# An encoder layer on one core: one ring of eight PSUM banks from the merge on, instead of rings of six and two

## The chip, the cores and the metric

The kernel runs on one core of one Trainium2 chip. The metric is the device time of one execution in microseconds (us); smaller is better. TensorE (PE in the profile) multiplies matrices and can write only to PSUM, which on this core is divided into eight banks of 128 partitions by 512 fp32 values. VectorE (DVE) and ScalarE (ACT) read the banks out; GpSimd (POOL) works on what they have put into SBUF; SyncE (SP) issues the DMA transfers. Each engine works through its own queue in order, and waits at the head of that queue for what its next instruction needs.

## The reference

One encoder layer is applied to two sequences of 512 tokens with 1024 features, with one set of weights, and a last normalization follows. Cut to the parts that matter here:

```python
def _rmsnorm(x, g):
    xf = x.astype(jnp.float32)
    y = xf * lax.rsqrt(jnp.mean(xf * xf, axis=-1, keepdims=True) + EPS)
    return (y * g.astype(jnp.float32)).astype(x.dtype)

def _layer(x, mem, l, p):
    xn = _rmsnorm(x, p['norm_mix'][l])
    ...                                   # S5 scan, differential attention, cross attention
    for n in range(N_BRANCH):
        term = jax.nn.sigmoid(g[..., n * D_MODEL:(n + 1) * D_MODEL]) * (branches[n] @ p['w_up'][l, n])
        merged = term if merged is None else merged + term
    x = x + merged @ p['w_out'][l]
    xn2 = _rmsnorm(x, p['norm_ffn'][l])
    gate, up = jnp.split(xn2 @ p['w_ffn_in'][l], 2, axis=-1)
    return x + (jax.nn.silu(gate) * up) @ p['w_ffn_out'][l]

def _trunk(x, mem, p):
    ...
    return _rmsnorm(x, p['norm_final'])
```

All is fp32, the feed-forward width is 2816, and the result is the normalized x of both sequences.

## The kernel before

**Products.** Features lie on the partitions and tokens on the free axis. Every fp32 operand is split into a high and a low part (`split`: a rounded copy on ScalarE and a subtraction on VectorE, L134 and L135), and a product is the sum of three matmuls per block of 128 features: high by high, high by low, low by high. The sum is collected in one PSUM bank. All matmuls are issued at L66, all transposes (a small matrix by the identity) at L69.

**The stages after the attention.** From L929 on stand, in this order: the merge of the second sequence (`merge_units`), the out projection (`out_tile`, which also sums up the squares of the new x for the second norm), the feed-forward input product in 22 tiles of 128 columns of gate and of up (i from 0 to 21), the feed-forward output product in visits (the loop over `VISITS`), and an end part with the last rows of that product.

**A tile and a visit.** Both form two by two quadrants from seven products in place of eight. A tile from 1 to 20 forms its seven products one after the other, 12 matmuls each, each in a bank of its own. Tile 0 gets its operands piece by piece, so it opens six banks at once and forms a seventh product, `last`, behind them. Tile 21 and every visit open seven banks at once. In `quadrants` the banks are read in the order of the products: a copy on ScalarE (L1108), then additions on VectorE (`summed`, L1102) into u2, c11, u3, p1, c22, c21 and c12; the fifth product's bank is read twice. For a tile, c11 and c12 are called gf, c21 and c22 up.

**The norm of the feed-forward input** is applied behind the product. In tile 0, `rstd` (L186) sums the squares of each sequence over the partitions with matmuls against a column of ones into a bank `ss`; `factor` (L195) takes the square root on ScalarE (L198) and the reciprocal on VectorE (L199), and four transposes spread the result over a bank `bc`. `S.copy` (L1155) copies it into `accs[s]`, by which the tile's quadrants are multiplied (L1164 on VectorE, L1166 on GpSimd).

**The end part** (L1334 to L1370) goes over three groups of columns: the 512 tokens of the first sequence, then the first and the second half of the second. For each, eight products m = 0 to 7 are added to y (L1346), the squares are collected in `acc` (ScalarE L181; the addition at L182 on GpSimd, for the last m on VectorE), `column_sums` gives `ss` with matmuls against ones, and `final` (L1314) calls `factor` and multiplies y by the result. The last group sums m = 5, 6 and 7 straight from the squares (L1360).

**The banks.** `open_banks` closes the rings that are open and opens new ones; `bank(tag)` takes the next bank of a ring, and a first write into it waits for the readers of what was in it before. From L929 to the end there are two rings: "mm" of six banks for products, and "tr" of two, from which `aux()` takes a bank for `ss`, for `bc`, and for the seventh product of tile 21 and of each visit.

**Order.** A scheduler orders the instructions of each engine within the program by the data they need, by what its own estimates say is ready, and by the order in which a ring hands out its banks. While `PE.on` is true the matmuls keep the order in which they are written: that is so from tile 21 through the visits; in the tiles before, and in the end part, the scheduler chooses.

Of the kernel before, what the change touches and what calls it, by code (L numbers as in the profile page):

```python
# [72 lines left out]
def encoder(ctx: ExitStack, tc: tile.TileContext, a, out):  # L73
# [14 lines left out]
    def open_tags(es, side=None, **tags):  # L88

        for tag, n in tags.items():  # L90
            pools[tag] = es.enter_context(tc.tile_pool(name=tag, bufs=n, side=side, reuse_waits="tile"))

    def open_banks(**tags):

        bank_es.close()
        for tag, n in tags.items():
            pools[tag] = bank_es.enter_context(tc.tile_pool(name=tag, bufs=n, space=PSUM, reuse_waits="tile"))

    bank_es = ExitStack()

    open_tags(ctx, ld=4)
    xp_es, phase = ExitStack(), ExitStack()
# [6 lines left out]
    def bank(tag="mm"):  # L109
        return pools[tag].tile([P, 512], F32, tag=tag, name="bk" + tag)  # L110

    def aux():
        return bank("tr")


    ident = cst.tile([P, P], F32, name="ident")
# [14 lines left out]
    def split(hi, lo, src, scale=None):  # L131

        if scale is None:
            h = S.copy(hi, src)  # L134
            l_ = V.tensor_tensor(out=lo, in0=src, in1=hi.bitcast(F32), op=ALU.subtract)  # L135
        else:
            h = S.activation(out=hi, in_=src, func=AF.Copy, scale=scale)
            l_ = V.scalar_tensor_tensor(out=lo, in0=src, scalar=scale, in1=hi.bitcast(F32), op0=ALU.mult, op1=ALU.subtract)
        return h, l_
# [65 lines left out]


    open_banks(mm=4, tr=4)
    bD = drp.tile([3, 4, P, NT], F32, name="bD")
    gD = drp.tile([24, P, NT], F32, name="gD")
# [83 lines left out]
    def queued():  # L293

        return tc.issue_after(last_w.ins)
# [146 lines left out]
    def raw_in(raw, m, p, whole=True):  # L442

        f = slice(2 * p * P, (2 * p + 2) * P)
        nc.sync.dma_start(raw[:, 1:3], a["w_fo"][m, :, f].rearrange("p (a n) -> p a n", n=P))
        if whole:
            return nc.sync.dma_start(raw[:, 0::3], a["w_fo"][m + 4, :, f].rearrange("p (a n) -> p a n", n=P))
        f = slice((2 * p + 1) * P, (2 * p + 2) * P)
        return nc.sync.dma_start(raw[:, 3], a["w_fo"][m + 4, :, f])

    def raw_sums(raw):

        a21, a11, a12, a22 = (raw[:, i] for i in range(4))
        PO.tensor_tensor(out=a22, in0=a21, in1=a22, op=ALU.add)  # L454
        PO.tensor_tensor(out=a21, in0=a11, in1=a21, op=ALU.subtract)
        PO.tensor_tensor(out=a11, in0=a22, in1=a11, op=ALU.subtract)
        PO.tensor_tensor(out=a12, in0=a12, in1=a11, op=ALU.subtract)

    def prepare(es_, todo_):
        pq = es_.enter_context(tc.tile_pool(name="pq", bufs=1, side="right", reuse_waits="tile"))  # L460
        raws = []

        def load():
            if len(raws) < len(todo_):
                raws.append(pq.tile([P, 4, P], F32, tag="raw", name="raw", bufs=4))
                with queued():
                    raw_in(raws[-1], *todo_[len(raws) - 1][:2])

        def part(n_, j, w_):
            m, p, _ = todo_[n_]  # L470
            k = w_.shape[1]
            hl = pq.tile([P, k, 2, P], F32R, tag=f"hl{k}", name="hl", bufs=k // 2)
            split(hl[:, :, 0], hl[:, :, 1], w_, scale=0.5)
            nc.sync.dma_start(wD[m, p][:, j : j + k], hl.bitcast(F32))

        for _ in range(3):
            load()
        yield
        for n_, (m, p, k) in enumerate(todo_):
            load()  # L480
            if k == 7:
                part(n_, 4, raws[n_][:, 1:4])
            if k == 7 or n_ == 0:
                raw_sums(raws[n_])
                yield
            part(n_, 0, raws[n_])
            if n_ + 1 < len(todo_) and todo_[n_ + 1][2] == 4:
                raw_sums(raws[n_ + 1])
            yield
# [201 lines left out]
    for i in range(-AHEAD, len(steps) + 1):  # L691
# [14 lines left out]
        if 0 <= i < len(steps):  # L706
# [4 lines left out]
            tr = aux()  # L711
# [214 lines left out]
    ves.close()  # L926


    open_banks(mm=6, tr=2)  # L929
    open_tags(phase, ms=16)  # L930
    ves = ExitStack()
    open_tags(ves, z=6)
# [21 lines left out]
    def out_tile(m, s, w):  # L954
        cs = slice(s * L, (s + 1) * L)
        xr = slot("xr", [P, L], name="xr")
        nc.sync.dma_start(xr, a["xT"][s, :, m, :])
        ps = bank()
        for k in range(KD):
            mm3([ps], w[0], w[1], [(mgh[k][:, cs], mgl[k][:, cs])], k, KD)  # L960
        V.tensor_tensor(out=x1[m][:, cs], in0=ps, in1=xr, op=ALU.add)
        nc.sync.dma_start(x1D[m, :, cs], x1[m][:, cs])
        sum_sq(accs[s], x1[m][:, cs], m == 0)
# [39 lines left out]
    def weights4(i):  # L1003

        nonlocal last_w
        a1, a2 = (wp.tile([P, DM], F32, tag="wf", name="wf") for _ in range(2))
        nc.sync.dma_start(a1, a["w_fg"][i])
        last_w = nc.sync.dma_start(a2, a["w_fu"][i])
        res = {}

        def sp(pool, src, sfx, *names):
            n = len(names) * H
            nonlocal last_s
            wh, wl = (pool.tile([P, DM], F32R, tag=t_ + sfx, name=t_, bufs=2) for t_ in ("wh", "wl"))
            last_s = split(wh[:, :n], wl[:, :n], src)
            for j, nm in enumerate(names):
                res[nm] = (wh[:, j * H : (j + 1) * H], wl[:, j * H : (j + 1) * H])

        sp(wp, a1, "", "A11", "A12")
        sp(wp, a2[:, H:], "", "A22")  # L1020
        yield res
        s12, s34 = (slot("ld", name="ws") for _ in range(2))
        PO.tensor_tensor(out=s12[:, :H], in0=a2[:, :H], in1=a2[:, H:], op=ALU.add)
        PO.tensor_tensor(out=s12[:, H:], in0=s12[:, :H], in1=a1[:, :H], op=ALU.subtract)
        PO.tensor_tensor(out=s34[:, H:], in0=a1[:, H:], in1=s12[:, H:], op=ALU.subtract)
        PO.tensor_tensor(out=s34[:, :H], in0=a1[:, :H], in1=a2[:, :H], op=ALU.subtract)
        yield
        sp(aps, s12, "s", "S1", "S2")
        sp(aps, s34, "s", "S3", "S4")
        yield  # L1030
# [12 lines left out]
    for s in range(NS):  # L1043
        for m, w in zip((3, 7), ws):
            out_tile(m, s, w)
    phase.close()
    open_tags(phase, th1=2, tl1=2)
    w0 = weights4(0)
    res0 = next(w0)
# [68 lines left out]
    def act_pair(p, tag="ts", third=PO):  # L1118

        xa_, xb_ = slot("ld", name="fa"), slot("ld", name="fb")  # L1120
        nc.sync.dma_start(xa_, aD[2 * p])
        nc.sync.dma_start(xb_, aD[2 * p + 1])
        return xa_, xb_, quad_sums(xa_, xb_, tag, third)

    def all7(i):
        wg = weights4(i)
        with yielding(last_q):
            w = next(wg)
        with tc.issue_after(last_p.ins):
            for _ in wg:  # L1130
                pass
        return w

    nxt_w = res0
    for i in range(KFF):
        w = nxt_w or all7(i)
        nxt_w = None
        if i == 1:
            prep = prepare(pes, pieces[NPREP[0] : NPREP[1]])
            next(prep)  # L1140
        elif i == KFF - 3:
            assert next(prep, None) is None
            pes.close()
            open_tags(fes, side="right", tsa=1, tsb=1)
        if i == KFF - 1:
            with tc.issue_after(last_s[1].ins):
                acts = [act_pair(0, "tsa"), act_pair(1, "tsb", V)]
            PE.on = True

        ps = products(i, w)  # L1150
        p0 = next(ps)
        if i == 0:
            for s in range(NS):
                _, bc = rstd(accs[s], DM)
                S.copy(accs[s], bc)  # L1155
        gf0, gf1, up0, up1 = quadrants(ps, p0)
        ac = ap2.tile([P, NT], F32, tag="ac", name="ac")
        with ExitStack() as es_:
            if i == KFF - 2:
                nxt_w = all7(i + 1)  # L1160
                es_.enter_context(tc.issue_after(last_s[1].ins))
            for s, gf, up in ((0, gf0, up0), (1, gf1, up1)):
                cs = slice(s * L, (s + 1) * L)
                V.tensor_tensor(out=gf, in0=gf, in1=accs[s], op=ALU.mult)  # L1164
                last_t = S.activation(out=ac[:, cs], in_=gf, func=AF.Tanh, scale=0.5)  # L1165
                PO.tensor_tensor(out=up, in0=up, in1=accs[s], op=ALU.mult)  # L1166
                V.scalar_tensor_tensor(out=ac[:, cs], in0=ac[:, cs], scalar=1.0, in1=gf, op0=ALU.add, op1=ALU.mult)
                V.tensor_tensor(out=ac[:, cs], in0=ac[:, cs], in1=up, op=ALU.mult)
        nc.sync.dma_start(aD[i], ac)
        if 1 <= i < KFF - 3:  # L1170
            half_piece((last_t, last_sum))
# [621 lines left out]
```

## Time and profile before

| | us |
|---|---|
| median of 3 runs | 1599.68 |
| lowest and highest | 1599.19, 1600.62 |
| the profiled execution, own time | 1599.28 |
| the profiled execution, span | 1597.5 |

The profile shows one execution. Its span runs from the first to the last instruction; 1.78 us of that execution's time lie around it. A time in a row of the profile counts from the start of the span. A row of the timeline gives the start, the duration, the engine, the line, the operation with its output and inputs, their sizes, how many instructions the row stands for, and in brackets how long the engine had been idle before it and what ended that. A matmul's duration includes its passage through the array, so that matmuls overlap: what one costs in a row of them is the distance between two starts.

### The profile page before, as it was taken

The numbers are of one execution on the slowest core, as the hardware profiler recorded it, in microseconds if no ns is written. First come the engines' busy times: TensorE is split into PE (matmuls) and PEld (weight loads), VectorE is DVE, ScalarE is ACT, GpSimd is POOL, SyncE is SP. The second block draws the span as 40 slices with busy tenths as digits, with TensorE's granted clock in tenths as the row PEclk, the third lists the DMA queues.
The fourth block names the chain that finished last, engine by engine and source line by source line (L and its number), as shares of the span: only waits on it lengthen the run. The fifth ranks groups of instructions, "written<-read, shape, count | busy, mean of one in ns | idle before, by whom it ended". The sixth has DMA issues, their size and how long they took to land.

```text
span 1597.5 us, 21606 instructions
## 1 busy us (share of the span) xinstructions
PE 1579.1 (99%) x7838; PEld 1314.8 (82%) x7838; DVE 1163.7 (73%) x1856; ACT 636.8 (40%) x1140; POOL 542.6 (34%) x449
## 2 busy tenths in 40 slices
PE   9999999999999999999999999999999999999997
PEld 7888788888898789878878878888888888788877
DVE  7976997067774776775365578888898778998654
ACT  6544313265552465573123443323333224233323
POOL 0010100001333220300443366666665553444553
PEclk9999999999999999999999999999999999999999
DMA  9544523676762111253454432333332223985222
GB/s 366 174 159 152 175 94 123 182 261 213 262 224 102 46 55 40 73 178 133 138 190 140 144 108 89 123 122 129 119 116 109 81 91 115 355 332 196 75 67 106
DMA packets 104890, 237.84 MB, mean 149 GB/s; under 512 B 13520, under 2 KB 45008, under 8 KB 104784
## 3 DMA queue, kind: packets, MB, share of 16 engines
q1 hardware_dynamic: 104784, 236.47, 43.4%
q8 instruction: 61, 1.00, 0.2%
q14 instruction: 45, 0.37, 0.1%
HBM read 165.16 MB, written 71.27 MB: 148 GB/s over the span
## 4 chain that ended last, share of the span: by engine, by line
PE 89%; DVE 5%; issue 2%; DMA 2%; POOL 1%; ACT 1%; SPq 0%; POOLq 0%; DVEq 0%; ACTq 0%
PE bkmm L66 78%; PE bktr L66 3%; DVE tl L135 2%; PE bkoo L66 2%; PE bktr L69 2%; PE bksc L66 1%; PE bktr L1627 1%; PE bktr L1598 1%; PE bktr L1688 0%; PE bktr L1686 0%; PE bktr L1687 0%; PE bktr L1566 0%; DMA acc<-in_w_fo 0%; DMA mt<-in_memT 0%; DMA fl<-aD 0%
## 5 line engine op out<-in xcount | busy, mean ns | idle before, releaser
L66 PE MATMUL bkmm<-xh,wh 128*128 128x512 f32 x640 | 254.7, 398 | 0.0
L66 PE MATMUL bkmm<-xh,wl 128*128 128x512 f32 x640 | 251.1, 393 | 0.0
L66 PE MATMUL bkmm<-xl,wh 128*128 128x512 f32 x640 | 250.5, 391 | 0.0
L66 PE MATMUL bkmm<-tl,wh 128*128 128x512 f32 (+1 forms) x621 | 241.3, 389 | 1.4 <-DVE tl L135 1.4
L66 PE MATMUL bkmm<-th,wl 128*128 128x512 f32 (+1 forms) x621 | 241.1, 389 | 1.0 <-DVE wl L135 1.0
L66 PE MATMUL bkmm<-th,wh 128*128 128x512 f32 (+1 forms) x621 | 241.3, 389 | 0.0
L134 ACT CAST wh<-wf 128x1024 fp32r<-128x1024 f32 (+1 forms) x134 | 117.9, 880 | 220.8 <-PE bkmm L66 183.2
L135 DVE TENSOR_TENSOR wl<-wf,wh 128x1024 fp32r<-128x1024 f32 (+1 forms) x134 | 146.5, 1093 | 48.8 <-ACT wh L134 33.5
L66 PE MATMUL bkmm<-th,w 128*128 128x512 f32 x432 | 141.4, 392 | 3.5 <-DVE up L1102 2.0
L66 PEld LDWEIGHTS bkmm<-xh,wl 128*128 128x128 f32 x640 | 120.2, 188 | 26.6 <-issue 1.3
L66 PEld LDWEIGHTS bkmm<-xh,wh 128*128 128x128 f32 x640 | 120.4, 188 | 26.4 <-issue 3.4
L66 PEld LDWEIGHTS bkmm<-xl,wh 128*128 128x128 f32 x640 | 120.5, 188 | 22.6 <-issue 0.4
L66 PEld LDWEIGHTS bkmm<-tl,wh 128*128 128x128 f32 x621 | 116.6, 188 | 26.2 <-DVE tl L135 2.1
L66 PEld LDWEIGHTS bkmm<-th,wl 128*128 128x128 f32 x621 | 116.6, 188 | 25.6 <-DVE wl L135 1.9
L66 PEld LDWEIGHTS bkmm<-th,wh 128*128 128x128 f32 x621 | 116.6, 188 | 23.7
L1166 POOL TENSOR_TENSOR up<-up,acc 128x512 f32<-128x512 f32 x44 | 84.2, 1931 | 87.4 <-DVE up L1102 87.4
L454 POOL TENSOR_TENSOR raw<-raw 128x128 f32<-128x128 f32 x28 | 15.2, 546 | 285.0 <-DVE nb L545 206.5
L66 PEld LDWEIGHTS bkmm<-th,w 128*128 128x128 f32 x432 | 80.9, 188 | 24.9 <-DVE up L1102 4.5
L793 POOL TENSOR_TENSOR mg<-mg,gl 128x1024 f32<-128x1024 f32 x16 | 43.5, 2720 | 138.1 <-DVE gl L789 138.1
L66 PE MATMUL bkmm<-tl,w 128*128 128x512 f32 x216 | 84.2, 390 | 0.0
L66 PE MATMUL bkmm<-yh,wh 128*128 128x512 f32 x192 | 75.9, 397 | 0.8 <-DVE gl L789 0.8
L1165 ACT ACTIVATE ac<-gf 128x512 f32<-128x512 f32 x44 | 27.8, 633 | 122.5 <-DVE gf L1164 63.5
(651 smaller groups left out, 3580.8 us busy)
## 6 DMA issues: line engine op xcount, KB each, us to landing
wf<-in_w_in SPq DMA_DIRECT2D x40, 512.0 KB, 4.1
wD<-hl SPq DMA_DIRECT2D x28, 512.0 KB, 2.9
w<-wD SPq DMA_DIRECT2D x28, 512.0 KB, 4.8
gD<-gt SPq DMA_DIRECT2D x24, 512.0 KB, 2.8
gl<-gD SPq DMA_DIRECT2D x24, 512.0 KB, 3.4
wf<-in_w_fg SPq DMA_DIRECT2D x22, 512.0 KB, 3.7
wf<-in_w_fu SPq DMA_DIRECT2D x22, 512.0 KB, 3.6
aD<-ac SPq DMA_DIRECT2D x22, 512.0 KB, 3.0
```

Source lines behind the costliest of these rows:

```text
L66: return self.put(self.eng.matmul(*args, **kw))
L69: return self.put(self.eng.transpose(*args, **kw))
L134: h = S.copy(hi, src)
L135: l_ = V.tensor_tensor(out=lo, in0=src, in1=hi.bitcast(F32), op=ALU.subtract)
L454: PO.tensor_tensor(out=a22, in0=a21, in1=a22, op=ALU.add)
L793: PO.tensor_tensor(out=mg[m], in0=mg[m], in1=gt, op=ALU.add)
L1165: last_t = S.activation(out=ac[:, cs], in_=gf, func=AF.Tanh, scale=0.5)
L1166: PO.tensor_tensor(out=up, in0=up, in1=accs[s], op=ALU.mult)
L1598: PE.matmul(kp[64 * hf : 64 * hf + 48, g * 144 : (g + 1) * 144], l_[:, 2 * hf + g, :], o_[:, 4 * g4 + 2 * hf + g, :], start=(l_ is lr48), ...
L1627: PE.matmul(ps[:, g * P : (g + 1) * P], w_[:, gg * P : (gg + 1) * P], u_[:, 8 * o + gg, :], start=True, stop=True)
```

## The change

`open_banks` notes which rings are open, and `aux()` takes its bank from "tr" if there is such a ring and from "mm" otherwise. At the merge one ring of eight banks is opened. Before tile 0 the rings of six and two are opened, and before tile 1 one ring of eight again. So the merge of the second sequence, the out projection, tiles 1 to 21, the visits and the end part use one ring of eight, in which `ss`, `bc` and the seventh products stand in turn with all other products; tile 0 alone has six and two. Lines of the changed kernel stand 2 lower from the aux function on, 3 lower from L1047 on, and 4 lower from L1139 on.

```diff
@@ -93,10 +93,12 @@
     def open_banks(**tags):
 
         bank_es.close()
+        open_now.clear()
+        open_now.update(tags)
         for tag, n in tags.items():
             pools[tag] = bank_es.enter_context(tc.tile_pool(name=tag, bufs=n, space=PSUM, reuse_waits="tile"))
 
-    bank_es = ExitStack()
+    bank_es, open_now = ExitStack(), {}
 ...
     def aux():
-        return bank("tr")
+        return bank("tr" if "tr" in open_now else "mm")
 ...
-    open_banks(mm=6, tr=2)
+    open_banks(mm=8)
     open_tags(phase, ms=16)
 ...
     phase.close()
+    open_banks(mm=6, tr=2)
     open_tags(phase, th1=2, tl1=2)
 ...
         if i == 1:
+            open_banks(mm=8)
             prep = prepare(pes, pieces[NPREP[0] : NPREP[1]])
```

## The prediction

> **What bounds the kernel now.** I read the page first, for the share of each engine.
>
> ```profile
> span 1597.5 us, 21606 instructions
> PE 1579.1 (99%) x7838; PEld 1314.8 (82%) x7838; DVE 1163.7 (73%) x1856; ACT 636.8 (40%) x1140; POOL 542.6 (34%) x449
> ```
>
> PE is busy for 1579.1 of 1597.5 us. The change alters no matmul and adds none, so it can win only what PE idles, 18 us, and it can lose wherever it makes PE idle more. The second view is therefore the list of PE's waits, and in it the waits for a bank. That is a wait released by an engine that reads a bank: `summed` at L1102.
>
> ```profile
> PE bkmm L66 <- DVE up L1102: 2.0, 3, 1.0
> ```
>
> Three waits, 2.0 us together, the longest 1.0: this is what more banks in the ring could take away. The other waits of PE are for operands, and a bank more doesn't bring these earlier.
>
> The third source is the order in which the instructions of both built programs stand on each engine. There are the same instructions in both but for two activation table loads fewer on ACT, and SP's queue of transfers is unchanged. The merge, the out projection, tiles 1 to 20 and the visits have the same order on PE; only their banks differ. Two places differ in order: tile 0, and the end part. In both, matmuls for `ss` and `bc` stand elsewhere than before. What these are worth is worked out from the timeline of each place.
>
> **Merge, out projection and tiles 1 to 21.** None of the three waits lies there; they begin at 1375 us, in the visits. Cost and gain are nothing. The cover is the reading engines' lead, and if it were gone the cost would show as new waits for L1102.
>
> **Visits.** The rows of PE that hold the three waits, and two reads of VectorE ahead of the first:
>
> ```profile
> 1375.04 0.50 PE L66 MATMUL bkmm<-th,w 128*128 128x512 f32 x1 [1.00 <-DVE up L1102]
> ...
> 1423.54 0.50 PE L66 MATMUL bkmm<-th,w 128*128 128x512 f32 x1 [0.46 <-DVE up L1102]
> ...
> 1481.98 0.50 PE L66 MATMUL bkmm<-th,w 128*128 128x512 f32 x1 [0.58 <-DVE up L1102]
> ...
> 1372.93 0.67 DVE L1102 TENSOR_TENSOR p<-bkmm,u 128x512 f32<-128x512 f32 x1
> ...
> 1374.31 0.68 DVE L1102 TENSOR_TENSOR up<-bkmm,u 128x512 f32<-128x512 f32 x1
> ```
>
> Before, the six products take the six banks of "mm", so product j of a visit takes the bank of product j of the last visit; the fifth is read twice (p, then up), and is free at 1374.99. In one ring of eight, with seven products a visit, product j takes the bank of product j-1. The fifth then needs the fourth's read, which stands ahead of p and is over by 1372.93, while PE is there at 1374.04: that wait goes. But the sixth now takes the twice-read bank. PE reaches it three matmuls later (0.23 each, below), at 1374.7, and waits 0.3 for 1374.99. So 0.7 of the 1.00 are won, the whole of 0.46 and 0.58 (each is shorter than those 0.7), and about 0.1 for each restart saved (the next fence shows 0.50 in place of 0.39 for a first matmul): **-2.1 us**. The ends are -1.4 (each wait only moves on by half) and -2.9 (all of them go, and one of 0.4 for u with them).
>
> [...]
>
> **Tile 0.** It has rings of six and two before and after. But the changed kernel closes them behind it, and tile 1 takes its banks from the new ring. In the built order all work on `ss` and `bc` of tile 0 now stands ahead of tile 1's first product: after the last matmul of `last` come four transposes for the first sequence, the ones-matmuls of the second, its four transposes, then tile 1. Before, the second ones stood among the products at 956.67, and transposes at 965.54, inside tile 1:
>
> ```profile
> 955.64 0.50 PE L66 MATMUL bkmm<-tl,wh 128*128 128x512 f32 x1 [0.80 <-DVE tl L135]
> ...
> 956.67 0.95 PE L66 MATMUL bktr<-onec,acc 128*128 128x1 f32 x8
> ...
> 960.10 0.39 PE L66 MATMUL bkmm<-th,wl 128*128 128x512 f32 x1
> 960.33 0.39 PE L66 MATMUL bkmm<-th,wh 128*128 128x512 f32 x1
> ...
> 965.54 0.60 PE L69 MATMUL bktr<-ident,rs 128*128 128x128 f32 x4
> ...
> 951.05 4.54 DVE L135 TENSOR_TENSOR tl<-ts,th 128x1024 fp32r<-128x1024 f32 x2
> ...
> 956.11 1.29 DVE L135 TENSOR_TENSOR wl<-wf,wh 128x1024 fp32r<-128x1024 f32 x1
> 957.33 0.68 DVE L1102 TENSOR_TENSOR u<-bkmm,p 128x512 f32<-128x512 f32 x1
> 957.93 0.76 DVE L1164 TENSOR_TENSOR gf<-gf,acc 128x512 f32<-128x512 f32 x1
> ...
> 960.94 0.95 DVE L135 TENSOR_TENSOR wl<-wf,wh 128x512 fp32r<-128x512 f32 x1
> ...
> 962.68 0.17 DVE L199 RECIPROCAL rs<-rs 128x4 f32<-128x4 f32 x1
> 962.77 1.25 DVE L1102 TENSOR_TENSOR up<-bkmm,u 128x512 f32<-128x512 f32 x2
> ```
>
> A matmul costs 0.23 (960.10 to 960.33). PE's work in front of the first transposes ends at about 959.8: 960.33, less 0.8 for the ones that moved behind, plus some 0.3 for ones of the first sequence that now stand here. The transposes need the reciprocal (L199). In VectorE's queue there stand between tl and that reciprocal four reads of banks at 0.60 (957.33 to 957.93), two wide splits at 1.22 (956.11 to 957.33), a narrow one at 0.87 (0.95 less the overlap of neighbours) and two reads at 1.2: 6.9 after 955.5, so 962.4, and 962.6 with the reciprocal's 0.17. PE waits **2.8**. Transposes 0.36 and ones 0.81 (both by the next fence) follow up to 963.8. The second reciprocal stands behind one more read, one split and L1164, 0.60, 1.22 and 0.7 after 962.5: about 965.1. PE waits **1.35** more, transposes at 965.2, and tile 1 starts at 965.55 in place of 960.33. Of these 5.2 us 0.36 were paid at 965.54 before: **+4.85**. Queued behind PE's waits is the whole of tile 1, so nothing hides them; VectorE and GpSimd only gain lead. Ends: +2, if VectorE takes its reads two places earlier than I walked, and +6, if it runs all wide splits and reads at full duration.
>
> **The end part.** In the one ring the `ss` and `bc` of a column group come between its last product and the next group's first, and PE's built order is: the first group's last product, ones, transposes, all 96 matmuls of the second group, ones, half of the third group's first six products, transposes, its other half, ones, two products, the last ones. Before, each stood some 40 matmuls later, with its input ready. Rows of before:
>
> ```profile
> 1561.65 0.39 PE L66 MATMUL bkmm<-r,tl 128*128 128x512 f32 x1
> 1561.87 0.28 PE L66 MATMUL bkmm<-th,wh 128*128 128x256 f32 x1
> ...
> 1566.91 0.95 PE L66 MATMUL bktr<-onec,acc 128*128 128x1 f32 x8
> 1567.72 0.36 PE L66 MATMUL bkmm<-th 128*128 128x256 f32 x1
> ...
> 1570.67 0.60 PE L69 MATMUL bktr<-ident,rs 128*128 128x128 f32 x4
> 1571.02 0.37 PE L66 MATMUL bkmm<-th 128*128 128x256 f32 x1
> ...
> 1574.69 0.28 PE L66 MATMUL bkmm<-th,wh 128*128 128x256 f32 x1
> ...
> 1587.56 0.37 PE L66 MATMUL bkmm<-r,tl 128*128 128x256 f32 x1
> ...
> 1588.95 0.61 PE L66 MATMUL bktr<-onec,nsq 128*128 128x1 f32 x4 [0.68 <-ACT nsq L1360]
> 1590.20 0.40 PE L69 MATMUL bktr<-ident,rs 128*128 128x128 f32 x2 [0.64 <-DVE rs L199]
> ...
> 1562.14 0.69 DVE L1346 TENSOR_TENSOR y<-y,bkmm 128x512 f32<-128x512 f32 x1 [2.10 <-PE bkmm L66]
> ...
> 1563.85 0.68 DVE L182 TENSOR_TENSOR acc<-acc,nsq 128x512 f32<-128x512 f32 x1
> ...
> 1579.55 0.42 DVE L182 TENSOR_TENSOR acc<-acc,nsq 128x256 f32<-128x256 f32 x1
> ...
> 1562.93 0.63 ACT L181 ACTIVATE nsq<-y 128x512 f32<-128x512 f32 x1 [2.16 <-DVE y L1346]
> ...
> 1583.17 0.73 POOL L182 TENSOR_TENSOR acc<-acc,nsq 128x256 f32<-128x256 f32 x1 [0.52 <-ACT nsq L181]
> ...
> 1587.04 2.78 POOL L1323 TENSOR_TENSOR y<-y,acc 128x256 f32<-128x256 f32 x4 [3.13 <-ACT acc L1320]
> ```
>
> First group: the addition ends at 1562.83, the square at 1563.56, the sum at 1564.3, then ones at 1564.35. From ones to transposes this very chain takes 1.25 in the last group (1588.95 to 1590.20), 1.6 with ones of 0.95 in place of 0.61: transposes at 1565.95, and the second group at 1566.3 in place of 1561.87. Of these 4.4 us before pays 0.81 and 0.36 later: +3.25. Second group: from the end of its last product to ones the last group shows 1587.68 to 1588.95, 1.25, and the sum at L182 adds 0.4: +1.65. Third group: the transposes start GpSimd's four scalings (2.78) at about 1585.1, ahead of three sums at 0.73 in its queue, and the last of these is done at 1590.05; PE is there at 1588.85: +1.2. The rest is a chain that ends the same way. **+6.1**; ends +4 (GpSimd's part hidden, 0.6 less at the first two) and +7.
>
> **The sum** against the profiled execution's own 1599.28 (span 1597.5 and 1.78 around it): 4.85 + 6.1 - 2.1 = +8.85, so 1608.1; against the median, 1599.68, it would be 0.4 more. I take **1608**.
>
> **Rivals.** *The stalls don't come* (faster): if the sums and reciprocals are ready when PE's queue reaches them, only the visits' gain is left, 1597.2 from 1599.28. It decides at VectorE's reciprocal: by 959.8 in tile 0, by 1562 in the end. For it speaks that VectorE is busy for 73% only; against it that the first group's sum can't precede its last product, whatever VectorE does. 0.06.
>
> *The clock falls in the new pauses.* Two windows of before, columns: busy time of PE, PEld, DVE, ACT, POOL, the granted clock, DMA:
>
> ```profile
> 1591.50:1591.80 0.30, 0.00 (x0) 0.00 (x0) 0.30 (x2) 0.00 (x0) 0.30 (x2) 1.00 0.19 58
> 1592.00:1592.50 0.50, 0.00 (x0) 0.00 (x0) 0.50 (x2) 0.00 (x0) 0.50 (x2) 0.50 0.00 0
> ```
>
> The granted clock falls to 0.50 at about 1591.9, 3.9 us after the last product's end (1587.93), although ones and transposes stand between. In the walk tile 0 has 5.75 us without a product, and the first group 4.3. If the clock falls after 3.9 and comes back 3.9 after products resume, those run at half speed and lose 1.95 at each place: 1610 with one, 1612 with both. [...] The trace agrees that it falls, and shows no recovery. That window's phase is open, so 0.27.
>
> *Only one place pays.* Only the end: +6.1 - 2.1, 1603.3, 0.08. Only tile 0: +4.85 - 2.1, 1602.0, 0.04.
>
> *The change doesn't do what it says:* reopening rings could make the new one wait like the old, and nothing else move: 1599.5, 0.05. In the built program only single banks are waited for, which speaks against it.
>
> **How the numbers follow.** The walked case has 0.50. A measurement here tells about 0.2% from no change, 3.2 us. Faster is the first rival, 0.06; same is 0.04 + 0.05 = 0.09; slower is the rest, 0.85. From 1603, which takes in the end alone and the low ends of the two stalls (+2 + 4 - 2.1), to 1612, which holds the high ends (+6 + 7 - 1.4) and the clock twice, some 0.17 is left out.
>
> **What would show it.** Right: PE's list has new waits on L199, L182 and the chain behind it at 959.8, 1562, 1578 and 1589, and the sum for L1102 falls from 2.0 to below 0.6. Tile 1's first product starts 5.2 later than before. The windows show whether the clock stays at 1.00 behind tile 0. Wrong: no wait over 1 us there, or a wait for L1102 in tiles 1 to 20.

## The result, and the profile after

The changed kernel takes 1614.12 us (median of 5 runs, 1613.80 to 1614.84) against 1599.68: slower, by a ratio of 1.0084 on record (95% interval 1.0074 to 1.0095); the medians alone give 1.0090. The forecast of slower held; the size did not: +14.4 against +8.3 (1608), and above the range's end of 1612. The profiled execution took 1613.80 us, 14.5 more than that of before. Lines of this kernel stand 2 to 4 lower than those of before: the reciprocal L199 is L201, the sum of squares L182 is L184, the addition L1102 is L1105.

The head of the page after, and from the list of TensorE's waits (engine, line, what was waited for: total us, times, longest) the lines that are new or changed:

```profile
span 1612.0 us, 21582 instructions
PE 1585.2 (98%) x7838; PEld 1319.8 (82%) x7838; DVE 1162.2 (72%) x1856; ACT 638.4 (40%) x1138; POOL 544.1 (34%) x449
```

```profile
PE bkmm L66 <- DVE acc L184: 3.9, 2, 2.4
PE bktr L69 <- DVE rs L201: 3.3, 2, 2.5
...
PE bkmm L66 <- POOL acc L184: 1.4, 1, 1.4
...
PE bkmm L69 <- DVE rs L201: 1.1, 2, 0.6
...
PE bkmm L66 <- DVE up L1105: 0.8, 1, 0.8
```

Every wait that the prediction named is there: for the reciprocal in tile 0 (3.3 in two), for the sums of the first and second group (3.9 in two), for GpSimd's sum in the third (1.4). The bank waits in the visits fell from 2.0 to 0.8. But PE's busy time, with the same 7838 matmuls, rose by 6.1 us. No wait explains that. The timeline of tile 0 does:

```profile
959.48 0.39 PE L66 MATMUL bkmm<-th,wl 128*128 128x512 f32 x1
962.38 0.65 PE L69 MATMUL bktr<-ident,rs 128*128 128x128 f32 x4 [2.51 <-DVE rs L201]
962.86 1.43 PE L66 MATMUL bktr<-onec,acc 128*128 128x1 f32 x8
965.09 1.11 PE L69 MATMUL bktr<-ident,rs 128*128 128x128 f32 x4 [0.80 <-DVE rs L201]
965.86 0.78 PE L66 MATMUL bkmm<-th,wh 128*128 128x512 f32 x1
966.43 0.63 PE L66 MATMUL bkmm<-tl,wh 128*128 128x512 f32 x1
966.86 0.63 PE L66 MATMUL bkmm<-th,wl 128*128 128x512 f32 x1
...
970.15 0.39 PE L66 MATMUL bkmm<-tl,wh 128*128 128x512 f32 x1
970.38 0.39 PE L66 MATMUL bkmm<-th,wl 128*128 128x512 f32 x1
```

The last product of `last` starts at 959.48, and tile 1's first at 965.86, where 965.55 was walked. But from there on a matmul costs 0.43 (966.43 to 966.86) until about 970, then 0.23 again: half clock. The view by windows (busy time of PE, PEld, DVE, ACT, POOL, then the granted clock, DMA share, GB/s) dates it, here and in the end part:

```profile
962.00:964.00 2.00, 1.62 (x12) 1.63 (x12) 2.00 (x4) 0.59 (x1) 2.00 (x4) 0.79 0.81 258
964.00:966.00 2.00, 1.20 (x7) 1.11 (x6) 1.04 (x3) 1.64 (x3) 2.00 (x4) 0.50 0.01 4
...
968.00:970.00 2.00, 2.00 (x6) 1.52 (x6) 1.37 (x1) 0.00 (x0) 2.00 (x3) 0.50 0.00 0
970.00:972.00 2.00, 2.00 (x11) 1.62 (x10) 2.00 (x2) 0.00 (x0) 2.00 (x2) 1.00 0.00 0
...
1570.00:1572.00 2.00, 1.43 (x8) 1.35 (x8) 0.26 (x2) 0.26 (x1) 0.00 (x0) 0.68 0.00 0
...
1574.00:1576.00 2.00, 2.00 (x19) 2.00 (x18) 2.00 (x4) 0.00 (x0) 0.00 (x0) 0.96 0.87 339
...
1584.00:1588.00 4.00, 2.45 (x20) 2.25 (x19) 1.01 (x3) 1.70 (x4) 0.73 (x1) 0.97 0.00 0
1588.00:1592.00 4.00, 4.00 (x24) 4.00 (x24) 0.84 (x2) 1.48 (x4) 0.09 (x1) 0.60 0.00 0
```

The clock fell three times: at about 963.2 until 970 (6.8 us), 1570.7 until 1574.2 (3.4) and 1587.8 until 1591.2 (3.4). In the 3.41 us ahead of each fall, as long as each of the two shorter stretches, PE was busy for 0.90, 1.05 and 1.86 us:

```profile
959.75:963.16 3.41, 0.90 (x9) 0.79 (x8) 3.41 (x7) 1.13 (x2) 3.41 (x7) 1.00 0.31 88
1567.32:1570.73 3.41, 1.05 (x8) 0.97 (x8) 1.12 (x3) 2.18 (x3) 0.00 (x0) 1.00 0.00 0
1584.39:1587.80 3.41, 1.86 (x16) 1.82 (x16) 1.01 (x3) 1.31 (x4) 0.45 (x1) 1.00 0.00 0
```

In the end part:

```profile
1566.39 0.39 PE L66 MATMUL bkmm<-r,tl 128*128 128x512 f32 x1
1569.14 1.05 PE L66 MATMUL bkmm<-onec,acc 128*128 128x1 f32 x8 [2.37 <-DVE acc L184]
1570.76 1.12 PE L69 MATMUL bkmm<-ident,rs 128*128 128x128 f32 x4 [0.57 <-DVE rs L201]
1571.53 0.56 PE L66 MATMUL bkmm<-th,wh 128*128 128x256 f32 x1
...
1585.98 0.61 PE L66 MATMUL bkmm<-onec,acc 128*128 128x1 f32 x4 [1.55 <-DVE acc L184]
...
1598.41 0.61 PE L66 MATMUL bkmm<-onec,acc 128*128 128x1 f32 x4 [1.37 <-POOL acc L184]
...
1602.16 0.28 PE L66 MATMUL bkmm<-r,tl 128*128 128x256 f32 x1
```

From the first group's last product to the last product it is 35.8 us (1566.39 to 1602.16), against 25.9 before (1561.65 to 1587.56): +9.9. Matmul by matmul the two traces lie 0.3 apart ahead of tile 0 (the changed kernel earlier) and 7.0 (later) behind tile 1, 4.7 at the first group's last product, 14.6 at the end. So in this execution tile 0 costs 7.3, the visits give back 2.3, the end part costs 9.9. A second trace of the same kernel, further down, divides the loss otherwise.

### The profile page after: what moved, and what is told of

It is laid out like the page before. It is cut to its first block, busy times and chain, and to the rows that moved or that the text cites. A ratio compares the mean times of both kernels' runs of the same rounds, so it can differ in the third digit from the quotient of the medians.

```text
span 1612.0 us, 21582 instructions
## 1 busy us (share of the span) xinstructions
PE 1585.2 (98%) x7838; PEld 1319.8 (82%) x7838; DVE 1162.2 (72%) x1856; ACT 638.4 (40%) x1138; POOL 544.1 (34%) x449
## 4 chain that ended last, share of the span: by engine, by line
PE 87%; issue 4%; DVE 3%; POOL 2%; DMA 2%; ACT 1%; SPq 0%; POOLq 0%; DVEq 0%; ACTq 0%
PE bkmm L66 77%; PE bktr L66 2%; PE bkoo L66 2%; PE bktr L69 2%; PE bksc L66 1%; DVE tl L137 1%; PE bktr L1631 1%; DMA yt<-bD 1%; POOL mg L795 1%; POOL y L1279 1%; PE bktr L1602 1%; PE bktr L1691 0%; PE bktr L1692 0%; PE bktr L1690 0%; PE bktr L1570 0%
## 5 line engine op out<-in xcount | busy, mean ns | idle before, releaser
L66 PE MATMUL bkmm<-th,w 128*128 128x512 f32 x504 | 157.3, 391 | 2.4 <-DVE up L1105 0.8
L66 PEld LDWEIGHTS bkmm<-th,w 128*128 128x128 f32 x504 | 94.3, 188 | 25.6 <-DVE w L140 1.7
L66 PE MATMUL bkmm<-tl,w 128*128 128x512 f32 x252 | 98.1, 389 | 0.0
L136 ACT CAST wh<-ws 128x1024 fp32r<-128x1024 f32 x44 | 46.3, 1053 | 87.2 <-PE bkmm L66 52.9
```

The costliest lines, as they stand in the source:

```text
L66: return self.put(self.eng.matmul(*args, **kw))
```

## The experiments

The theory: PE pauses in tile 0 and in the end, because small matmuls that wait for sums and reciprocals stand in front of products; the pauses make the clock fall; the visits gain 2.1. Kernels measured together ran on one chip with their own runs of before: medians 1600.39, 1600.61 and 1600.55 for the three groups. Their single runs spread wider (1598.1 to 1605.5 for before), so places are read from the traces. A trace is one execution.

**The end part given back its two rings.**

```diff
     PE.on = False
+    open_banks(mm=6, tr=2)
     def ones(ss, sq, n, start=False, stop=False):
```

> The changed kernel with rings of six and two opened again for the end part. Theory: tile 0's +6.7 and the visits' -2.1 stay, the end's +9.9 goes: 1604.3; the clock is low behind tile 0 only. Rival (the end waits for its data whatever the rings are): still about 1614. Rival (closing a ring costs by itself, as it may in tile 0): a new wait of 2 us or more at the first product of the end part, 1606 to 1608.

Measured: 1605.60 against 1600.39, ratio 1.0034 (1.0022 to 1.0047), so +5.2, 1.3 above what was expected. No wait for L184 is left, and no low clock in the end but the last. The end's loss is that of the one ring. In tile 0 the clock was low from 956.1 to 962.9: not behind the pause, as expected, but ahead of it.

**The head given back its rings.** One ring of eight from the first visit on; six and two ahead of it.

```diff
-    open_banks(mm=8)                  # at the merge; the two lines at tiles 0 and 1 go too
+    open_banks(mm=6, tr=2)
...
     n_p = 0
+    open_banks(mm=8)
     for v, (m, lo_, hi_) in enumerate(VISITS):
```

> Rings of six and two as before through tile 21; one ring of eight for the visits and the end part only. Theory (TensorE pauses in tile 0 and in the end part, each with a stretch of half clock behind it, less the visits' gain): the end keeps its +9.9 (the shift of the last product less that at the first group's end, 14.6 - 4.7), the visits their -2.1, tile 0's +6.7 goes: 1599.7 + 7.8 = 1607.5, with the granted clock at 0.50 in two stretches of the end and nowhere else before the last chain. Rival (one ring of eight costs in the merge and in tiles 1 to 20 as well, by bank traffic): more than 6.7 goes, below 1606. Rival (the clock falls for a reason of its own, at the same times in any kernel): a low stretch about 963 to 970 remains, and the time is about 1609.5.

Measured: 1614.69, ratio 1.0088 (1.0074 to 1.0101). Missed by 7 us, and the experiment was flawed: the new ring starts at its first bank, whatever tile 21 left in it, and the first visit waited 1.68 us for a read. Its trace is also 2.8 us late ahead of the visits, where the kernel is that of before, and its end part costs 11.1. The next kernel shows the flaw better.

**The ring of eight for the visits alone**, with the end given back as well.

> Before, with one ring of eight for the visits alone, six and two for all else; TensorE's order is that of before throughout. Theory: the visits' gain alone, -2.1: 1597.6, the sum of waits for the bank reads at the addition falls from 2.0 to 0.8 or less. Rival (the waits in the visits are set by VectorE's lateness and only move on): within 0.5 of 1599.7.

Measured: 1608.42, ratio 1.0046 (1.0033 to 1.0059), where 1597.6 was expected. From its list of waits:

```profile
PE bkmm L66 <- DVE u L1104: 3.9, 1, 3.9
PE bkmm L66 <- DVE gf L1104: 2.0, 1, 2.0
```

Its trace, too, is 2.7 us late ahead of the visits. The second wait is the first visit's, at 1367.65; the first wait is that of the end part's first product, at 1547.08, whose bank in the reopened ring is the one that the last visit's fourth product was read from late, with half clock behind it. Closing a ring is not free: it forgets whose turn it is. Neither theory nor rival had that.

**Fillers.** Products that nobody reads stand in the pauses; the order of all else is that of the changed kernel.

```diff
+    def fill_bank(b_, count):
+        for j in range(count):
+            PE.matmul(b_, filler[0], filler[1], start=(j == 0), stop=(j == count - 1))
...
         bc = aux()
+        fill_bank(bc, room)           # tile 0: 10 and 3
...
         ss = aux()
+        fill_bank(ss, 9 if n == L else 6)
         ones(ss, acc, n, True, True)
```

> The changed kernel with products that nobody reads put into the pauses, in TensorE's order: 10 and 3 of 512 columns before the two sets of transposes of tile 0 (2.3 and 0.7 us), 9 and 6 before the ones-matmuls of the first and second group of the end (2.1 and 1.4 us); they write the bank that the next step overwrites, and the order of everything else is that of the changed kernel. Theory (the pauses make the clock fall, and the half clock costs about 1.9 us behind tile 0 and about 3 us in the end): the stalls stay, as the fillers fit into them, the granted clock stays at 1.00 up to the last chain, and the time falls by 4.5 to 5.5, to about 1609. Rival (the stalls alone make the loss, the half clock is hidden): within 1 us of 1614. Rival (fillers delay the chain): above 1614.

Measured: 1615.60 (1611.19 to 1617.61), no faster; the rival that fillers delay the chain had said above 1614. Its trace is that of a short execution (1611.55):

```profile
962.40 0.16 DVE L207 RECIPROCAL rs<-rs 128x4 f32<-128x4 f32 x1
...
962.54 2.43 PE L66 MATMUL bktr<-th,wh 128*128 128x512 f32 x10
964.81 0.60 PE L69 MATMUL bktr<-ident,rs 128*128 128x128 f32 x4
...
1565.72 0.39 PE L66 MATMUL bkmm<-r,tl 128*128 128x512 f32 x1
...
1584.29 0.37 PE L66 MATMUL bkmm<-th,wh 128*128 128x256 f32 x1
```

The low stretches behind `last`, behind the first and behind the second group are gone, and the end part is shorter: from the first group's last product to the third group's first it is 18.6 us (1565.72 to 1584.29) against 20.1 (1566.39 to 1586.45). But the clock was low from 954.2 to 961.1 at the start of tile 0, where PE waits for operands, and from 1595.9, behind the third group's pause, which had no fillers. That the fillers moved the falls there isn't shown: the second trace of the changed kernel, without a filler, has low stretches in both places (956.2 and 1601.3). And in tile 0 the fillers stood in the way: the first reciprocal was ready at 962.56, and its transposes started at 964.81, behind ten fillers. The third group's pause got five too (`fill_bank(ss, 5)` at m = 5):

> The changed kernel with the fillers in all four pauses that had them, and five more (1.1 us) in the pause of the third group, before its ones-matmuls, where the kernel with four pauses filled still waited 1.35 and then ran its last two products at half clock. Theory (a stretch of low use makes the clock fall, wherever the 3.4 us window happens to fall; each fall costs about 1.5 to 2): the end part has no low stretch before its last chain, and the time from the first group's last product to the last product is about 31.5, against 35.8 in the changed kernel; a low stretch at the start of tile 0 may remain, where TensorE waits for operands, so 1609 to 1613 in all. Rival (fillers do not keep the clock up): a low stretch in the end as in the changed kernel, and 35 or more.

Measured: 1612.81 (1609.17 to 1616.82). The end part of its trace, and the windows in which the changed kernel had run at half clock:

```profile
1566.80 0.39 PE L66 MATMUL bkmm<-r,tl 128*128 128x512 f32 x1
1567.02 2.20 PE L66 MATMUL bkmm<-th 128*128 128x512 f32 x9
1569.56 1.05 PE L66 MATMUL bkmm<-onec,acc 128*128 128x1 f32 x8 [0.33 <-DVE acc L184]
...
1599.62 0.28 PE L66 MATMUL bkmm<-r,tl 128*128 128x256 f32 x1
```

```profile
1570.00:1574.00 4.00, 3.43 (x30) 3.35 (x30) 2.31 (x5) 0.27 (x2) 0.00 (x0) 1.00 0.00 0
1588.00:1592.00 4.00, 4.00 (x36) 4.00 (x35) 2.09 (x5) 2.63 (x6) 2.12 (x3) 1.00 0.00 0
```

No low stretch, and 32.8 us (1566.80 to 1599.62) in place of 35.8. The ones still start when the sum is there (2.76 behind the first group's last product, 2.75 in the changed kernel), so the 3.0 saved are the price of the two falls, 1.5 each; 6.9 of the end's 9.9 are stalls in the wider sense, waits and what small matmuls displace. The 31.5 expected had put the price of a fall higher. The total lies in the 1609 to 1613 expected; tile 0 kept a low stretch, from 955.2 to 962.0.

**The rings of tile 0 closed one tile later**, with the end given back.

```diff
-        if i == 1:
+        if i == 2:
             open_banks(mm=8)
+        if i == 1:
             prep = prepare(pes, pieces[NPREP[0] : NPREP[1]])
```

> The changed kernel with the rings of tile 0 closed before tile 2 in place of tile 1, and with rings of six and two again for the end part. TensorE's order at the end is that of before, and the transposes of tile 0 stand among products again. Unlike the kernel with the ring for the visits alone, which opened its ring between tile 21 and the first visit and met a bank still being read (1.98 us), and met another at the end (3.9), here the ring turns through from tile 2 to the last visit and the first product of the end finds a free bank. Theory: tile 0's +6.7 and the end's +9.9 both go, the visits' -2.1 is left: 1597.6 to 1598.5, low clock in the last chain only. Rival (closing rings costs wherever it is done): a new wait at the first product of tile 2, and 1600 or more. Rival (a ring of eight costs in the merge and in tiles 2 to 20): 1600 or more without such a wait.

Measured: 1602.53, ratio 1.0014 (1.0005 to 1.0023): the waits behind `last` are gone, and yet it is 1.9 above before, where 1597.6 to 1598.5 was expected. Its tile 0, in the shortest of eleven executions (1600.61), by PE's waits and by windows:

```profile
953.07 0.49 PE L66 MATMUL bkmm<-th,wh 128*128 128x512 f32 x1 [0.82 <-ACT th L136]
...
956.38 0.79 PE L66 MATMUL bkmm<-tl,wh 128*128 128x512 f32 x1 [1.03 <-DVE tl L137]
```

```profile
954.00:958.00 4.00, 2.82 (x8) 2.00 (x9) 4.00 (x4) 2.11 (x3) 4.00 (x4) 0.71 0.52 141
958.00:962.00 4.00, 4.00 (x13) 3.32 (x12) 3.90 (x6) 0.26 (x1) 4.00 (x7) 0.50 0.43 131
```

With the rings opened anew before tile 0, the first sequence's ones stand some 60 matmuls later than before, PE comes to the operands that are not ready with less work done in between, and the clock falls there, behind a window in which PE was busy for 1.71 of 3.41 us (952.23 to 955.64; 2.61 in before, 953.58 to 956.99). In this trace tile 0 costs 4.0 by that alone: it is 0.8 later than before ahead of tile 0 and 4.8 behind tile 2. The theory didn't have that. The rival that the ring of eight costs in the merge or in tiles 2 to 20 would give such a total, but the trace stays 4.8 later from behind tile 2 up to the visits, so nothing is lost there. The other traces agree: of the seven traces with rings opened anew before tile 0, six have a low stretch that starts between 954 and 957, and the five with tile 0 as before have none in tile 0.

**The same without giving back the end.**

> The changed kernel with the rings of tile 0 closed before tile 2, and nothing else: the end part keeps the one ring. Theory: tile 0's +6.7 goes, the end's +9.9 stays: 14.4 - 6.7 above before, 1607.5 to 1608.5; two stretches of half clock in the end, none at 960 to 970. Rival (the half clock of the end costs nothing, the end's loss is smaller): below 1606. Rival (the division itself costs, not its closing before tile 1): about 1614.

Measured: 1613.03, ratio 1.0074 (1.0061 to 1.0088). 10.5 above the last kernel: the end's loss again. It is 4.5 above what was expected, as tile 0's loss did not all go: its trace has the low stretch there from 955.0 to 961.8.

Beside them ran the changed kernel once more:

> The changed kernel itself, on the chip of the three beside it, as their yardstick. By its first runs 14.4 above before: 1614 to 1615 where before is 1599.7 to 1600.4.

Measured: 1615.97, ratio 1.0093 (1.0079 to 1.0108), 1 above what was expected. In this second trace the loss divides otherwise: it is 1.8 later than before ahead of tile 0, tile 0 costs 5.7, the visits give back 1.7, and the end part costs 10.9 (36.8 us from the first group's last product, at 1567.48, to the last product, at 1604.27). Its tile 0, and the windows ahead of and in the low stretch there:

```profile
964.42 0.65 PE L69 MATMUL bktr<-ident,rs 128*128 128x128 f32 x4
...
968.00 0.65 PE L69 MATMUL bktr<-ident,rs 128*128 128x128 f32 x4 [2.14 <-DVE rs L201]
968.41 0.48 PE L66 MATMUL bkmm<-th,wh 128*128 128x512 f32 x1
```

```profile
952.79:956.21 3.42, 2.01 (x10) 1.18 (x8) 3.42 (x3) 2.48 (x3) 3.34 (x3) 1.00 0.53 145
956.21:963.03 6.82, 5.78 (x16) 4.65 (x16) 6.71 (x9) 1.93 (x3) 6.82 (x9) 0.50 0.40 120
```

The clock falls ahead of the pause, TensorE comes to the first transposes when their reciprocal is ready, and only the second set waits. In the end part the clock is low from 1570.6 to 1577.4 and from 1601.3 to 1604.7, behind the first and the third group. So where the clock falls differs between two executions of one kernel.

**No division at tile 0**: the two lines at tiles 0 and 1 removed, one ring from the merge to the end.

> The changed kernel without the division at tile 0: one ring of eight from the merge to the end. In the built order the four transposes of the first sequence, the ones and the transposes of the second still stand back to back in tile 0, 10 products behind the first ones. Theory (what costs is that sums and transposes stand in front of products that have no need of them): tile 0 pays about as much as in the changed kernel, 5 to 8, and the time is 1612 to 1616. Rival (the division of tile 0, by its closing, is what costs there): 1607 to 1609.

Measured: 1617.33, ratio 1.0105 (1.0091 to 1.0119), above the range that I gave. In tile 0 the second set of transposes waits alone for 4.95 us:

```profile
964.54 1.12 PE L69 MATMUL bkmm<-ident,rs 128*128 128x128 f32 x4 [4.95 <-DVE rs L201]
```

So leaving out the division at tile 0 wins nothing, and the rival (1607 to 1609) falls. That it costs more is not shown: the interval overlaps that of the changed kernel beside it.

**Tile 0 as before, the ring of eight from tile 2 on.** All lines of PE stand as before in the first kernel; the second lets the end keep the one ring.

```diff
-    open_banks(mm=8)                  # at the merge
+    open_banks(mm=6, tr=2)
...
-    open_banks(mm=6, tr=2)            # before tile 0
...
-        if i == 1:
+        if i == 2:
             open_banks(mm=8)
...
     PE.on = False
+    open_banks(mm=6, tr=2)            # the first kernel only
```

> Rings of six and two as before through tile 1, one ring of eight from tile 2 through the visits, six and two again in the end part. TensorE's order is that of before throughout, and the ring meets no bank that is still being read, at its opening or at the end. Theory (the ring of eight is worth its -2.1 in the visits; all losses come from the order in tile 0 and in the end, and from the half clock behind pauses): 1.5 to 2.5 below before, with the waits for the addition's reads at 0.8 or less and no stretch of half clock but the last. Rival (a ring of eight costs in tiles 2 to 20, or the ring's changes cost wherever they are made): no faster than before, or slower.

> As the kernel beside it, but the end part keeps the one ring: tile 0 as before, so the end's loss stands alone. Theory: stalls of about 6 to 7 and two or three stretches of half clock at about 1.5 each, +9.9, with the visits' -2.1: 7 to 9 above before. Rival (part of the end's loss was brought along from tile 0): under 6 above before.

Measured: 1599.08 against 1600.55, ratio 0.9990 (0.9980 to 0.9999), for the first, and 1608.28, ratio 1.0046 (1.0034 to 1.0059), for the second. The first is the version that beats both, though only just clear of no change: -1.5 by the medians. Matmul by matmul its trace, the shortest of its eleven executions (1596.19), is 2.7 ahead of before at 1523.73 in the visits. Its waits for bank reads:

```profile
PE bkmm L66 <- DVE up L1104: 0.9, 2, 0.4
```

The second has the end's loss alone: +7.7 as expected, 9.2 more than the first.

## Why the prediction was right and wrong

**Visits: the number right, its parts only partly.** -2.1 was predicted; the two traces of the changed kernel have -2.3 and -1.7, and a kernel with nothing else is 1.5 faster. But the waits at the addition fell from 2.0 to 0.8, and to 1.2 in the second trace, not below 0.6. The rest of the 2.3 came mostly with shorter waits for operands (wl 1.0 to 0.5, ScalarE's w 0.7 to 0.3), of which the prediction had said that a bank more doesn't bring them earlier: as far as the prediction goes, that part was luck. **Merge, out projection, tiles 2 to 20: right** that the ring is worth nothing there and costs nothing.

**Tile 0: the mechanism right in part, the places where it begins and ends wrong.** In the first trace the two waits, walked as 2.8 and 1.35, are 2.51 and 0.80, the second shorter because its ones ran slower (1.43 for the eight); tile 1 starts 0.3 from where it was put. But the step "+4.85" ends at tile 1's first product, and the loss goes on to 970. And it begins at `last`: that opening the rings anew before tile 0 moves the first sequence's ones, and costs by itself, was not walked. By the medians that part is 3.4 (the kernel closed one tile later, +1.9, against -1.5 for the one from tile 2 on), and closing before tile 1 adds 3.3 (5.2 less 1.9).

**The end part: mechanism right, size slightly low.** Stalls +6.1 predicted, 6.9 by the filled kernel.

**The failed step is that the clock stood outside the sum, as a rival: its chance and its size.** The fall of the clock was put at nothing in the sum and kept as a rival with 0.27, at 1.95 a place and two places at most. In the profiled execution the clock fell at three places. Its share there is 3.0 in the end, and in tile 0 about 2.3, an estimate from the rows: between 965.86 and 970 some 9.7 matmuls cost 0.43 in place of 0.23, and the second transposes take 0.77 (965.09 to 965.86) in place of the 0.41 of the second trace (968.00 to 968.41). That is 5.3 in all, against the 5.7 by which the sum of 8.85 lay below +14.5; the stalls and the visits differ from their terms by the rest. In the second trace, too, the clock was low at three places, for 6.8, 6.8 and 3.4 us. By the medians the +14.4 is made up of 9.2 for the end (1608.28 less 1599.08), 3.4 and 3.3 for tile 0, and -1.5 for the visits, each good to some 2 us.

Two things were misread. I took the 3.9 us between the last product and the fall, in before, for a delay that a pause must last; the second group's pause is 2.0 without a product (1584.43 to 1586.45), and the clock fell behind it. And in tile 0 it stayed low for 6.8 us, not 3.9. That it comes back after 3.9 was my assumption: no run shows it, nor did the trace of before show the window that the 0.27 speaks of; the low stretches lasted 6.8, 3.4 and 3.4. The range's end is too low by the prediction's own terms: the high ends alone give 1610.9 and the clock twice on the middle sum 1612.0, but both together 1614.8.

In the first trace of the changed kernel the ends of the low stretches (969.98, 1574.14 and 1591.21) lie a whole number of 3.41 us apart: 17.07 is five of 3.414, 604.16 is 177 of 3.413. What sets that spacing is not shown. The longest idle gap of TensorE ahead of a fall is 2.51, and the clock fell behind stretches of 3.41 us with PE busy for 27%, 31% and 55%. A safe share isn't shown: in the kernel with the end given back the clock fell at 956.10 behind a stretch at 59%, and stayed up behind one at 54%, the second stretch of that length after its return at 962.93:

```profile
952.69:956.10 3.41, 2.01 (x11) 1.44 (x10) 3.41 (x3) 2.48 (x3) 3.33 (x2) 1.00 0.41 103
966.34:969.76 3.42, 1.85 (x10) 1.62 (x11) 2.80 (x4) 2.66 (x4) 3.42 (x4) 1.00 0.01 2
```

**Other rivals.** "The stalls don't come" fell with the list of waits. "Only one place pays" fell: 5.2 above before with the end given back, 7.7 with tile 0 given back. "The change doesn't do what it says" fell too. But what that rival played down, that opening a ring has a cost of its own, is real: up to 3.9 us in the kernel with the ring for the visits alone, and 3.4 in tile 0 through the order. At tile 1 of the changed kernel the new ring happened to meet free banks: there is no wait for L1105 there.

## What to carry to other kernels

A ring that mixes long products with small matmuls that wait for a chain of other engines turns allocation order into queue order: the small ones block an in-order engine until their data is there, so a ring of their own for two banks can be worth more than two more banks for products (here the one ring lost 9.2 us in the end part and won 1.5 in the visits). When a stall on TensorE is priced, the granted clock behind it belongs in the sum and not among the rivals (an estimated 5.3 of the 14.5 us here): look at the busy share of the 3.4 us behind which it fell here, 27% to 59%, and not only at the longest gap, 2.51 in the first trace. Where a ring is closed and opened anew, see which bank comes first and who still reads it (waits of 2.0 and 3.9 us in the kernel with the ring for the visits alone).

## What the runs showed of the hardware

In the first trace of the changed kernel the granted clock fell from 1.00 to 0.50 behind stretches of 3.41 us in which TensorE was busy for 27%, 31% and 55%, and was back at 1.00 after 6.8 us in tile 0 and after 3.4 us, twice, in the end part; a matmul of 512 columns cost 0.43 us at 0.50 and 0.23 at 1.00, and each fall in the end part cost about 1.5 us. What share of work keeps the clock up stays open, as in one trace a stretch at 54% passed without a fall and one at 59% did not. Two executions of the changed kernel had their falls at different places (963.2, 1570.7 and 1587.8 in one, 956.2, 1570.6 and 1601.3 in the other), and of thirteen traces the eight in which tile 0's order of matmuls had changed have a low stretch there, the other five none. What set the spread of single runs (1598.1 to 1605.5 for before) was not traced, and stays open.
